# The low part of every split issued before the functions that hang on a step's end

## The chip, the cores and the metric

The kernel runs on one core of one Trainium2 chip. The metric is the time of one execution on the device in microseconds, as the median of several runs. A profiled execution of the same program gives the trace that all rows here are read from.

## What is computed

The reference is a decoder trunk of two layers over 256 tokens of width 2048, in float32. The first layer mixes with a gated recurrence (RG-LRU) and causal pooling, the second with sparse attention in three branches; both then have a squared-ReLU MLP of width 8192 and a gated addition of a per-layer embedding, and a norm closes the whole. Cut to what the change touches:

```python
hn = rmsnorm(h, ln_mlp_g[i])
h = h + jnp.square(jax.nn.relu(hn @ mlp_w_up[i])) @ mlp_w_down[i]
gate = jax.nn.sigmoid(rmsnorm(h, ln_ple_g[i]) @ ple_w_gate[i])
h = h + gate * (p[i] @ ple_w_proj[i])
...
return rmsnorm(h, ln_final_g)      # after both layers
```

The mixers are `ab_mixer` (projection, causal convolution of four taps, two gates per head, a scan over time, pooling, projection) and `nsa_mixer` (projection, compression of keys and values, softmax over the compressed, selected and windowed keys, projection).

## The kernel before

Every matmul multiplies float32 numbers as two parts of a rounded type: a **high part**, which ScalarE makes by copying 128 x 1024 raw weights into the rounded type (`emit_hi`, L204), and a **low part**, which VectorE makes by subtracting the high part from the raw weights (`emit_lo`, L211). TensorE then runs three products for each pair of tiles: high x high and high x low of the activations, and low x high (L704, L705, L706 in the large sets; L294, L298, L299 in the others). The weights, 1 MB a load, come in by SyncE's queue.

The program is a list of **steps**. A step takes half a load (two tiles of 128 rows), and `run()` (from L249) writes the code for one step after the other. The order of the code is the order on each engine: nothing is rescheduled. For step s it issues, before the change, in this order: sums of weights for step s+4 where a set needs them (`emit_sum`), the high part for step s+2, the low part of step s if it isn't there yet, the step's matmuls (`fn`), then the functions that were put down for the end of this step, and last the low part for step s+2.

`after(n, fn)` puts a function down for the end of the n-th step from now; everything that turns a finished set of matmuls into the next input goes that way: the additions, relus and squares of the MLP, the transposes, the scans, the softmax, the Tanhs. A step of twelve matmuls is TensorE's unit of time, and a function put down for the next step comes one step later on every engine.

The large sets (`mm_set`) do a matrix of 128 x 8 by 512 in a Strassen-like scheme: products p over sums of blocks, with results kept in 8 PSUM banks, and some products moved out to SBUF tiles (`u` and `big`, L760 to L770) in the course of the set. `column()` gives the last product of a set; its `by_n` tells that one of the two column blocks n is complete. At the end of an **up set** of the MLP (`up_out`, from L925; 16 of them, two layers of four quarters of two halves) there are two column blocks of 512, n = 0 and 1. For each: `adds` (L932, VectorE, two operations, from PSUM into `u` and `big`), `relu` (L936 and L938 on ScalarE, two relus and two squares), and then `back`, the transposes on TensorE (L807) that read the squares, `u` and `big` by turns, followed by copies and subtractions that split them.

The **gate sets** of the second layer (`gate`, from L1006) end in `last`: two Tanhs on ScalarE (L1023), on VectorE an addition with product and an addition to the stream `h` for each token tile t (L1027, L1028), a square with a running sum on ScalarE (L1067), and products by the gain of the final norm (L1031). The very last call of it is followed by `finish`, which takes the root of the mean square (L1072) and writes the output. Ahead of the last squares an activation of one column, `warm` (L1025), makes the table of the root load early.

## Time and profile before

| what | value |
|---|---|
| median of 3 runs | 2303.78 us (2302.41 to 2306.06) |
| the profiled execution | 2306.73 us |
| its span in the trace | 2304.7 us |
| mean granted clock of TensorE | 0.996 of full speed |
| TensorE (PE) busy | 2277.0 us, 99%, 11510 matmuls |
| weight loads (PEld) busy | 1933.8 us, 84% |
| VectorE (DVE) busy | 1734.8 us, 75% |
| ScalarE (ACT) busy | 1315.6 us, 57% |
| chain that ended last | TensorE 97%, VectorE 1%, ScalarE 1% |

Read it from the top: TensorE is the engine that sets the time, and the chain of work that ended last runs on it almost all through. The other two are busy for much of the time beside it, VectorE most of all with low parts (L211, 817 + 128 of them, 1098 us), but their busy time is not on the path. Each engine runs its own list in order and halts at an instruction whose input isn't there; what stands behind it halts too.

### The profile page before, as it was taken

To read this page: it belongs to the slowest core of one execution; us is meant where nothing else is said; L and a number is where in the kernel's file an instruction comes from. 1 tells how busy PE (TensorE), PEld (TensorE's weight loads), DVE (VectorE), ACT (ScalarE), POOL (GpSimd) and SP (SyncE) were. 2 spreads that over 40 slices of the span, in tenths; PEclk is the share of its full clock that TensorE was granted. 3 is DMA by queue.
4 is the path that set the end of the run, shared out by engine and by line. 5 is a ranking of instruction groups with operands and counts; after the bars stand their busy time and mean duration, and the time that the engine had idled before them with its cause. 6 is when DMAs were issued, how large, how long until landed. Compare 5 with 4: busy or idle time off the path is not lost.

```text
span 2304.7 us, 30201 instructions
## 1 busy us (share of the span) xinstructions
PE 2277.0 (99%) x11510; PEld 1933.8 (84%) x11510; DVE 1734.8 (75%) x2365; ACT 1315.6 (57%) x1903; POOL 14.5 (1%) x42
## 2 busy tenths in 40 slices
PE   8999999999999999999999999999999999999997
PEld 8998888888888888889889988888888888888875
DVE  6786688788788787756775675687877877877864
ACT  6665465565565565665564554566456556556563
POOL 2000000000000000000000000000000000000000
PEclk9999999999999999999999999999999999999998
DMA  7545556556555555555775224555555555555553
GB/s 258 212 157 184 197 182 213 189 182 212 190 183 209 193 181 201 199 175 201 268 263 178 83 85 162 187 187 197 201 187 197 200 186 198 201 185 198 207 175 111
DMA packets 69537, 436.56 MB, mean 189 GB/s; under 512 B 9872, under 2 KB 14352, under 8 KB 18448
## 3 DMA queue, kind: packets, MB, share of 16 engines
q1 hardware_dynamic: 64832, 427.90, 53.3%
q10 hardware_dynamic: 4560, 6.74, 0.9%
q8 instruction: 90, 1.47, 0.3%
q14 instruction: 55, 0.45, 0.1%
HBM read 432.51 MB, written 2.10 MB: 189 GB/s over the span
## 4 chain that ended last, share of the span: by engine, by line
PE 97%; DVE 1%; ACT 1%; DMA 0%; issue 0%; SPq 0%; DVEq 0%; ACTq 0%
PE ps L706 25%; PE ps L704 25%; PE ps L705 25%; PE ps L294 11%; PE ps L298 3%; PE ps L807 2%; PE ps L299 1%; PE ps L1378 1%; PE ps L1168 1%; DVE lo L211 0%; DMA raw<-in_ab_w_in 0%; PE ps L1320 0%; PE ps L1318 0%; PE ps L960 0%; PE ps L587 0%; PE ps L1321 0%
## 5 line engine op out<-in xcount | busy, mean ns | idle before, releaser
L204 ACT ACTIVATE hi<-raw 128x1024 fp32r<-128x1024 f32 (+1 forms) x817 | 819.0, 1015 | 475.5 <-PE ps L705 390.0
L211 DVE TENSOR_TENSOR lo<-raw,hi 128x1024 fp32r<-128x1024 f32 (+1 forms) x817 | 941.2, 1165 | 193.9 <-ACT hi L204 193.4
L704 PE MATMUL ps<-hi,big 128*128 128x512 f32 x2496 | 978.3, 392 | 0.0
L706 PE MATMUL ps<-lo,big 128*128 128x512 f32 x2496 | 973.2, 390 | 4.8 <-DVE lo L211 4.8
L705 PE MATMUL ps<-hi,big 128*128 128x512 f32 x2496 | 973.0, 390 | 0.0
L706 PEld LDWEIGHTS ps<-lo,big 128*128 128x128 f32 x2496 | 469.4, 188 | 103.9 <-DVE lo L211 6.1
L705 PEld LDWEIGHTS ps<-hi,big 128*128 128x128 f32 x2496 | 469.5, 188 | 95.6
L704 PEld LDWEIGHTS ps<-hi,big 128*128 128x128 f32 x2496 | 469.3, 188 | 95.3
L294 PE MATMUL ps<-big,hi 128*128 128x256 f32 x1408 | 265.8, 290 | 6.7 <-ACT hi L204 6.4
L204 ACT ACTIVATE hi<-big 128x1024 fp32r<-128x1024 f32 x128 | 135.8, 1061 | 212.2 <-PE ps L705 198.6
L211 DVE TENSOR_TENSOR lo<-big,hi 128x1024 fp32r<-128x1024 f32 x128 | 156.5, 1223 | 120.2 <-ACT hi L204 120.2
L294 PEld LDWEIGHTS ps<-big,hi 128*128 128x128 f32 x1408 | 223.9, 194 | 9.1 <-ACT hi L204 6.4
L294 PE MATMUL ps<-big,lo 128*128 128x256 f32 x704 | 201.0, 286 | 1.2 <-DVE lo L211 1.2
L294 PEld LDWEIGHTS ps<-big,lo 128*128 128x128 f32 x704 | 136.3, 194 | 1.8 <-DVE lo L211 1.8
L298 PE MATMUL ps<-big,hi 128*128 128x512 f32 x320 | 113.7, 398 | 0.0
L299 PE MATMUL ps<-big,lo 128*128 128x256 f32 x320 | 89.7, 280 | 0.6 <-DVE lo L211 0.5
L735 DVE TENSOR_TENSOR big<-raw 128x1024 f32<-128x1024 f32 x64 | 77.9, 1218 | 0.0
L298 PEld LDWEIGHTS ps<-big,hi 128*128 128x128 f32 x320 | 60.1, 188 | 14.2
L950 DVE TENSOR_TENSOR big<-ps,big 128x512 fp32r<-128x512 f32 x64 | 41.1, 684 | 36.6 <-ACT big L946 36.6
L299 PEld LDWEIGHTS ps<-big,lo 128*128 128x128 f32 x320 | 60.4, 189 | 2.0 <-DVE lo L211 1.5
L410 ACT ACTIVATE big<-ps,gains 128x256 fp32r<-128x256 f32 x80 | 31.2, 471 | 42.6 <-PE ps L807 42.6
L866 DVE SCALAR_TENSOR_TENSOR big<-ps,gains,big 128x256 fp32r<-128x256 f32 x80 | 33.2, 476 | 25.1 <-ACT big L410 20.4
(249 smaller groups left out, 1514.5 us busy)
## 6 DMA issues: line engine op xcount, KB each, us to landing
raw<-in_mlp_w_up SPq DMA_DIRECT2D x128, 1024.0 KB, 4.9
raw<-in_mlp_w_down SPq DMA_DIRECT2D x128, 1024.0 KB, 4.9
raw<-in_c_w_in SPq DMA_DIRECT2D x36, 1024.0 KB, 4.9
raw<-in_ple_w_gate SPq DMA_DIRECT2D x32, 1024.0 KB, 4.9
raw<-in_ab_w_in SPq DMA_DIRECT2D x20, 1024.0 KB, 4.9
raw<-in_ab_w_out SPq DMA_DIRECT2D x16, 1024.0 KB, 4.9
raw<-in_c_w_out SPq DMA_DIRECT2D x16, 1024.0 KB, 4.9
raw<-in_c_cmp_w_k SPq DMA_DIRECT2D x8, 1024.0 KB, 5.0
```

Source lines behind the costliest of these rows:

```text
L204: act.activation(halves[s]["hi"][:, k, :w], halves[s]["src"][:, k, :], AF.Copy)
L211: dve.tensor_tensor(lo[:, k, :w], src[:, k, :], halves[s]["hi"][:, k, :w].bitcast(F32), op=OP.subtract)
L294: pe.matmul(b, lhsT=wt[:, kk, cols], rhs=x[:, x0:x0 + T], start=first and n == 0 and j % 2 == 0, stop=last and n == 2, skip_group_check=True)
L298: pe.matmul(b, lhsT=hi[:, kk, cols], rhs=x, start=first, stop=False, skip_group_check=True)
L299: pe.matmul(b[:, T:], lhsT=lo[:, kk, cols], rhs=x[:, :T], start=False, stop=last, skip_group_check=True)
L704: pe.matmul(b, lhsT=x_hi, rhs=hi[:, n, :], start=r not in begun, stop=False, skip_group_check=True)
L705: pe.matmul(b, lhsT=x_lo, rhs=hi[:, n, :], start=False, stop=False, skip_group_check=True)
L706: pe.matmul(b, lhsT=x_hi, rhs=lo[:, n, :], start=False, stop=end, skip_group_check=True)
L735: dve.tensor_tensor(t, raw[:, 0::3, :], raw[:, 1:2, :].to_broadcast([P, 2, 512]), op=OP.add)
L807: pe.transpose(b[:, j, t * P:(t + 1) * P], of(t, i // 2, (2 * i + j) % 4), ident)
L866: dve.scalar_tensor_tensor(X(k)[:, T:], scratch(banks, i)[:, j], gain(k), X(k)[:, :T].bitcast(F32), op0=OP.mult, op1=OP.subtract)
L950: dve.tensor_tensor(Hs[n2][:, k:k + 2, T:], scratch(banks, i), Hs[n2][:, k:k + 2, :T].bitcast(F32), op=OP.subtract)
```

## The change

Three things change. In `run()` the low part for step s+2 is issued right behind the matmuls of step s, ahead of the functions put down for the step's end; these are then called until none is left for this step, so that one of them can put down another for the same step. In `column()` the call of `by_n` becomes such a function. And in the gate sets of the second layer the work of `last` is dealt out: the second column block comes two steps behind the first instead of one, the additions of token tile 1 come one step behind those of tile 0, and the products by the gain later or with them; the early load of the root's table is taken out.

```diff
--- before.py
+++ after.py
@@ -255,10 +255,11 @@
             splits("hi", ahead)
             splits("lo", s)
             fn(halves[s]["hi"], halves[s]["lo"])
+            splits("lo", ahead)
             now = state["step"]
-            for f in later.pop(now, []):
-                f()
-            splits("lo", ahead)
+            while now in later:
+                for f in later.pop(now):
+                    f()
             state["step"] += 1
             halves[s].clear()
         while later:
@@ -776,7 +777,7 @@
                     for t in range(2):
                         product(PLAIN[t][n], A(p, k, t), hi, lo, k, k == 1 and p == order[-1])
                 if p == order[-1]:
-                    by_n(n, [acc_of(PLAIN[t][n]) for t in range(2)])
+                    after(0, lambda: by_n(n, [acc_of(PLAIN[t][n]) for t in range(2)]))
             return fn
 
         for i, p in enumerate(order):
@@ -1021,21 +1022,30 @@
                 end = n2 == 1 and n == 1
                 for t in range(2):
                     act.activation(W[t][:, n], banks[t], AF.Tanh, scale=HALF[:, t:t + 1])
-                if end:
-                    act.activation(warm, epsb, AF.Sqrt)
-                for t in range(2):
+
+                def add(t):
                     dve.scalar_tensor_tensor(W[t][:, n], W[t][:, n], 1.0, eb(t, n), op0=OP.add, op1=OP.mult)
                     dve.tensor_tensor(hb(t, n), hb(t, n), W[t][:, n], op=OP.add)
                     last_square(t, n2, n)
-                for t in range(0 if end else 2):
+
+                def times_gain(t):
                     dve.tensor_tensor(hg(t, n), hb(t, n), gb(n), op=OP.mult)
                 if end:
+                    add(0)
+                    add(1)
                     finish()
+                    return
+                for t in range(2):
+                    after(t, lambda t=t: add(t))
+                    if n2 == 0:
+                        after(4 + 2 * n + t, lambda t=t: times_gain(t))
+                    else:
+                        after(t, lambda t=t: times_gain(t))
 
             def post(w, banks):
                 if l == 1:
                     for n in range(2):
-                        after(n, lambda n=n: last(n, [banks[t][n] for t in range(2)]))
+                        after(2 * n, lambda n=n: last(n, [banks[t][n] for t in range(2)]))
                     return
                 W = wtiles()
 
```

VectorE at the end of an up set, before; `lo` is a low part, named by its tile's number, with the raw weights and the high part that it reads, and L932 are the additions of block 0 and then of block 1:

```order
L761 TENSOR_TENSOR u_3250<-ps_1968,u_3250 128x512
L211 TENSOR_TENSOR lo_3255<-raw_3154,hi_3242 128x1024
L765 SCALAR_TENSOR_TENSOR big_2268<-big_2268,u_3250 128x512
L766 TENSOR_TENSOR u_3250<-u_3250,big_2268 128x512
L211 TENSOR_TENSOR lo_3275<-raw_3177,hi_3259 128x1024
L770 SCALAR_TENSOR_TENSOR big_2268<-big_2268 128x512
L932 TENSOR_TENSOR u_3250<-ps_2277,u_3250 128x512
L932 TENSOR_TENSOR big_2268<-ps_2282,big_2268 128x512
L211 TENSOR_TENSOR lo_3298<-raw_3177,hi_3277 128x1024
L932 TENSOR_TENSOR u_3250<-ps_2281,u_3250 128x512
L932 TENSOR_TENSOR big_2268<-ps_2289,big_2268 128x512
L211 TENSOR_TENSOR lo_3330<-raw_3230,hi_3302 128x1024
```

VectorE at the same place, with the change (the additions are L933 there):

```order
L211 TENSOR_TENSOR lo_3250<-raw_3154,hi_3242 128x1024
L762 TENSOR_TENSOR u_3252<-ps_1968,u_3252 128x512
L211 TENSOR_TENSOR lo_3273<-raw_3177,hi_3259 128x1024
L766 SCALAR_TENSOR_TENSOR big_2268<-big_2268,u_3252 128x512
L767 TENSOR_TENSOR u_3252<-u_3252,big_2268 128x512
L211 TENSOR_TENSOR lo_3291<-raw_3177,hi_3277 128x1024
L771 SCALAR_TENSOR_TENSOR big_2268<-big_2268 128x512
L933 TENSOR_TENSOR u_3252<-ps_2277,u_3252 128x512
L933 TENSOR_TENSOR big_2268<-ps_2282,big_2268 128x512
L211 TENSOR_TENSOR lo_3316<-raw_3230,hi_3302 128x1024
L933 TENSOR_TENSOR u_3252<-ps_2281,u_3252 128x512
L933 TENSOR_TENSOR big_2268<-ps_2289,big_2268 128x512
```

Each low part has moved up by one group of functions, so that one now stands between the two pairs of additions, and it reads `hi_3302`. On ScalarE, where that high part is made, the order is that of before; with the change, from the relus of block 0 to the squares of block 1:

```order
L937 ACTIVATE u_3252<-u_3252 128x512
L937 ACTIVATE big_2268<-big_2268 128x512
L939 ACTIVATE u_3252<-u_3252 128x512
L939 ACTIVATE big_2268<-big_2268 128x512
L204 ACTIVATE hi_3302<-raw_3230 128x1024
L937 ACTIVATE u_3252<-u_3252 128x512
L937 ACTIVATE big_2268<-big_2268 128x512
L939 ACTIVATE u_3252<-u_3252 128x512
L939 ACTIVATE big_2268<-big_2268 128x512
```

Nothing moved here: `hi_3302` stands behind the relus and squares of block 0, and ahead of those of block 1.

VectorE at the end of the second layer's first gate set (`h_79` is the stream, L1027 and L1028 the additions), before:

```order
L1027 SCALAR_TENSOR_TENSOR u_18224<-u_18224,big_17865 128x512
L1028 TENSOR_TENSOR h_79<-h_79,u_18224 128x512
L1027 SCALAR_TENSOR_TENSOR big_12316<-big_12316,big_17865 128x512
L1028 TENSOR_TENSOR h_79<-h_79,big_12316 128x512
L1031 TENSOR_TENSOR big_17867<-h_79,big_17866 128x512 x2
L211 TENSOR_TENSOR lo_18235<-raw_18124,hi_18210 128x1024
L1027 SCALAR_TENSOR_TENSOR u_18224<-u_18224,big_17865 128x512
L1028 TENSOR_TENSOR h_79<-h_79,u_18224 128x512
L1027 SCALAR_TENSOR_TENSOR big_12316<-big_12316,big_17865 128x512
L1028 TENSOR_TENSOR h_79<-h_79,big_12316 128x512
L1031 TENSOR_TENSOR big_17867<-h_79,big_17866 128x512 x2
L211 TENSOR_TENSOR lo_18263<-raw_18158,hi_18239 128x1024
```

and with the change:

```order
L211 TENSOR_TENSOR lo_18208<-raw_18124,hi_18194 128x1024
L211 TENSOR_TENSOR lo_18224<-raw_18124,hi_18210 128x1024
L1027 SCALAR_TENSOR_TENSOR u_18226<-u_18226,big_17865 128x512
L1028 TENSOR_TENSOR h_79<-h_79,u_18226 128x512
L211 TENSOR_TENSOR lo_18248<-raw_18158,hi_18234 128x1024
L1027 SCALAR_TENSOR_TENSOR big_12316<-big_12316,big_17865 128x512
L1028 TENSOR_TENSOR h_79<-h_79,big_12316 128x512
L211 TENSOR_TENSOR lo_18267<-raw_18158,hi_18253 128x1024
L1027 SCALAR_TENSOR_TENSOR u_18226<-u_18226,big_17865 128x512
L1028 TENSOR_TENSOR h_79<-h_79,u_18226 128x512
L211 TENSOR_TENSOR lo_18290<-raw_18192,hi_18276 128x1024
L1027 SCALAR_TENSOR_TENSOR big_12316<-big_12316,big_17865 128x512
```

The first low part stands ahead of the additions, a low part follows each further pair, and the products L1031 (L1032 with the change) stand further back.

ScalarE at the program's end, before:

```order
L1023 ACTIVATE u_18517<-ps_12325,rs_81 128x512
L1023 ACTIVATE big_12316<-ps_12330,rs_81 128x512
L1067 ACTIVATE jk_82,ssq_80<-h_79 128x512 x2
L1023 ACTIVATE u_18517<-ps_12329,rs_81 128x512
L1023 ACTIVATE big_12316<-ps_12337,rs_81 128x512
L1025 ACT_TABLE_LOAD
L1025 ACTIVATE warm_92<-epsb_88 128x1
L1067 ACTIVATE jk_82,ssq_80<-h_79 128x512 x2
L1072 ACTIVATE rs_81<-rs_81,epsb_88 128x2
L1080 ACTIVATE big_17867<-big_17867,rs_81 128x768 x2
```

and with the change:

```order
L1024 ACTIVATE u_18519<-ps_12325,rs_81 128x512
L1024 ACTIVATE big_12316<-ps_12330,rs_81 128x512
L1077 ACTIVATE jk_82,ssq_80<-h_79 128x512 x2
L1024 ACTIVATE u_18519<-ps_12329,rs_81 128x512
L1024 ACTIVATE big_12316<-ps_12337,rs_81 128x512
L1077 ACTIVATE jk_82,ssq_80<-h_79 128x512 x2
L1082 ACT_TABLE_LOAD
L1082 ACTIVATE rs_81<-rs_81,epsb_88 128x2
L1090 ACTIVATE big_17867<-big_17867,rs_81 128x768 x2
```

The load of the table has moved from behind the last Tanhs to behind the last squares, right ahead of the root.

## Rows read from the trace of the kernel before

**Rows 1.** The page's first part: TensorE's busy time and share of the span.

```profile
PE 2277.0 (99%) x11510; PEld 1933.8 (84%) x11510; DVE 1734.8 (75%) x2365; ACT 1315.6 (57%) x1903; POOL 14.5 (1%) x42
```

**Rows 2.** TensorE's waits: who waited for whom, us in total, times, longest.

```profile
PE ps L706 <- DVE lo L211: 4.8, 3, 2.1
PE ps L294 <- DVE lo L211: 1.2, 1, 1.2
PE ps L1356 <- DVE big L1352: 0.5, 1, 0.5
PE ps L299 <- DVE lo L211: 0.5, 1, 0.5
```

**Rows 3.** Timeline of TensorE at an up set's end: start, us, engine, line, operation.

```profile
345.42 0.27 PE L807 MATMUL ps<-ident,big 128*128 128x128 f32 x1
...
349.03 0.27 PE L807 MATMUL ps<-ident,big 128*128 128x128 f32 x1
```

**Rows 4.** Timeline of VectorE at the same end; in brackets, idle before and releaser.

```profile
336.73 0.69 DVE L761 TENSOR_TENSOR u<-ps,u 128x512 f32<-128x512 f32 x1 [0.88 <-PE ps L706]
337.34 1.22 DVE L211 TENSOR_TENSOR lo<-raw,hi 128x1024 fp32r<-128x1024 f32 x1
338.47 0.69 DVE L765 SCALAR_TENSOR_TENSOR big<-big,u 128x512 f32<-128x512 f32 x1
...
341.61 0.69 DVE L932 TENSOR_TENSOR u<-ps,u 128x512 f32<-128x512 f32 x1
```

**Rows 5.** Timeline of ScalarE at the same end.

```profile
336.95 2.01 ACT L204 ACTIVATE hi<-raw 128x1024 fp32r<-128x1024 f32 x2
...
343.98 0.62 ACT L938 ACTIVATE big<-big 128x512 f32<-128x512 f32 x1
344.50 1.04 ACT L204 ACTIVATE hi<-raw 128x1024 fp32r<-128x1024 f32 x1
...
347.01 0.62 ACT L938 ACTIVATE big<-big 128x512 f32<-128x512 f32 x1
```

**Rows 6.** Timeline of TensorE at the second layer's first gate set's end.

```profile
2233.00 0.39 PE L704 MATMUL ps<-hi,big 128*128 128x512 f32 x1
...
2235.72 0.39 PE L704 MATMUL ps<-hi,big 128*128 128x512 f32 x1
...
2242.15 0.50 PE L706 MATMUL ps<-lo,big 128*128 128x512 f32 x1 [2.07 <-DVE lo L211]
...
2246.82 0.39 PE L704 MATMUL ps<-hi,big 128*128 128x512 f32 x1
```

**Rows 7.** Stretches: us, TensorE busy (count), granted clock, DMA share, GB/s.

```profile
18.20:19.00 0.80, 0.80 (x6) 0.50 1.01 394
...
2244.00:2244.80 0.80, 0.80 (x3) 0.50 0.71 113
```

**Rows 8.** Timelines of VectorE and ScalarE in the recurrence.

```profile
94.58 0.43 DVE L543 TENSOR_TENSOR big<-big 128x256 f32<-128x256 f32 x1 [0.95 <-ACT big L540]
...
94.45 2.00 ACT L204 ACTIVATE hi<-raw 128x1024 fp32r<-128x1024 f32 x2
```

**Rows 9.** Timelines of VectorE and ScalarE at the last attention heads.

```profile
1383.71 1.28 DVE L1352 TENSOR_SCALAR big<-big,mz 128x128 f32<-128x128 f32 x6
...
1383.15 1.99 ACT L204 ACTIVATE hi<-raw 128x1024 fp32r<-128x1024 f32 x2
```

**Rows 10.** Timelines of TensorE and ScalarE at the end of the program.

```profile
2284.61 0.39 PE L705 MATMUL ps<-hi,big 128*128 128x512 f32 x1
...
2290.68 0.52 PE L706 MATMUL ps<-lo,big 128*128 128x512 f32 x1
...
2291.23 0.69 ACT L1023 ACTIVATE big<-ps,rs 128x512 f32<-128x512 f32 x1 [0.48 <-PE ps L706]
2291.94 1.28 ACT L1025 ACT_TABLE_LOAD   x1
...
2295.03 0.30 ACT L1072 ACTIVATE rs<-rs,epsb 128x2 f32<-128x2 f32 x1 [0.23 <-DVE rs L376]
```

## The prediction

> **What bounds the kernel now.** I read the busy shares first, then the list of waits, then the timelines of the places where the order of work changes. TensorE is busy 2277.0 us of the 2304.7 us span [rows 1], so an edit can gain little except where TensorE stands. Outside the ramp at the start and the tail its list of waits is short [rows 2]: three waits for a low part at L706 (4.8 us together), one at L294 (1.2), one for the scaled probabilities at L1356 (0.5), one at L299 (0.5). So nearly every result that VectorE and ScalarE make comes in time, and what the reader must ask of each move is not how long VectorE works but how near to its deadline the work was that now stands behind a low part.
>
> The pace: twelve matmuls, one plain step, go from 2233.00 to 2235.72, 2.72 us, 0.2268 each [rows 6]. A low part holds VectorE for 1.13 us, from its start at 337.34 to that of the next operation at 338.47 [rows 4]; a high part takes ScalarE 1.04 [rows 5].
>
> The profiled execution took 2306.73 us, the span and 2.03 around it; the median of the timed runs, 2303.78, is 2.95 below it. My sum is of differences, so I read it from the trace and put it on the median. A difference under 0.2%, 4.6 us, can't be told from none.
>
> **The change part by part.** No instruction is added but one load of a table that trades its place; TensorE's order stays. What moves is VectorE's: each low part goes ahead of the functions that hang on its step's end.
>
> *The end of an up set, 16 times (two layers, four quarters, two halves).* The code's order for VectorE becomes: additions for column block 0, low part, additions for block 1. The low part needs its high part, and that one stands on ScalarE behind the two relus and two squares of block 0, which need the additions of block 0. So block 1, which waited for none of this, now waits for all of it. By times: in the trace VectorE idles 0.88 us ahead of L761 at 336.73 [rows 4], so the first low part that is moved fits there for nothing. The next can't start at 337.34 as a low part did there: its high part is the first of the pair that begins at 336.95 on ScalarE and takes until 338.0 [rows 5], so it starts at about 338.03, 0.69 later, and everything up to the additions of block 0 moves from 341.61 to 342.30. The squares of block 0 end 2.99 us after the additions' start (341.61 to 344.60, the second square beginning at 343.98 and lasting 0.62), so now at 345.29; the transposes that need the last of them stood at 345.42 [rows 3]: just in time. The high part then ends 0.94 later, at 346.23; the low part runs 346.27 to 347.40; only there do the additions of block 1 start, and 2.99 later, at 350.39, their last square is done. The second transpose of that block, the first to read it, stood at 349.03 [rows 3]. It starts at 350.42: 1.39 us lost on TensorE, whose queue is in order. I find no cover: the other 15 sets have the same three orders, and the matmuls behind the transposes are TensorE's own. In the first set of each layer two more small operations stand in the chain, 1.86 there. Sum: 14 x 1.39 + 2 x 1.86 = **+23.2**. Bounds: 10 (if the high part gets to ScalarE some 0.8 earlier than I think) to 30 (if the transposes of block 0 come late too).
>
> *The recurrence, near 95 us.* The scans' products start at 94.58, right behind the square root on ScalarE; the high parts come behind that root, from 94.45 as a pair [rows 8]. The low part that now stands ahead ends near 96.6, so scans and all behind them come 2.1 later, and VectorE doesn't rest before the convolution that TensorE then takes up. Estimate from these: **+1.6**, between 0 and 2.1.
>
> *The attention's heads.* TensorE already waits for the scaling at L1356 [rows 2]. At the last pair the scaling begins at 1383.71 [rows 9]; a low part is put ahead of it whose high part begins at 1383.15, behind the exponentials, and so ends near 1384.2. Low part to 1385.4, the scaling's two small operations again, scaling at 1385.8: +2.1, all of it on TensorE, since the wait had no slack. The other heads have some slack; I put 1.2 on them. **+3.3**, between 1.5 and 6.
>
> *Start and 1115 us.* Here TensorE waits for the low part itself, 1.2 and 0.5 [rows 2]; it now stands ahead of two conversions of x or of a few additions. **-0.7** and **-0.5**, bounded by nothing and the whole wait.
>
> *The second layer's gate set, 2236 to 2247.* From 2235.72 to 2246.82 stand 27 matmul intervals, 11.10 us where 27 x 0.2268 = 6.12 would do: 4.98 lost, of which 2.07 is the one wait before 2242.15 [rows 6] and a good third the half-speed stretch that follows it, in which the granted clock is 0.50, the 1.2 GHz level [rows 7]. In the changed order the low parts of both waits stand ahead of the additions, so these waits go. But the dealt-out additions now take turns with low parts as in the up set: high part 1.04, low part 1.13, two additions 1.3, square 0.7 make 4.2 us a turn, where TensorE's step takes 2.72. Three turns are covered by the lead that the first low part gains; at the fourth and fifth TensorE waits 0.5 and 1.55. So 2.05 stay lost: **-2.9**, between 0 and -4.9.
>
> *The end.* Ten intervals from 2284.61 to 2290.68, 6.07 instead of 2.27 [rows 10], for the same reason; with the low part early the last matmul starts at 2286.88, and the last Tanh, at 2291.23 before, at 2287.30. VectorE's four operations behind the Tanhs, about 0.69 each [rows 4], end at 2290.09, the last square at 2290.85. Now the load of the root's table, 1.28, begun at 2291.94 before while VectorE worked [rows 10], stands bare ahead of the root: 2292.15 against 2295.03. **-2.9**; the lost cover costs 0.5 of it net, since in the old place the load held up a square. Bounds -1.5 and -4.2. The Trainium skill ("ScalarE: Activation LUTs", What ACT_TABLE_LOAD costs) has 1.28 us for the load, which this trace's 1.28 confirms, and adds a drain of about 1.38, which no row here shows; by it the tail would gain 1.5 and not 2.9, and the forecast would be 1.4 higher.
>
> Sum: 23.2 + 1.6 + 3.3 - 0.7 - 0.5 - 2.9 - 2.9 = **+21.1**; 2303.8 + 21.1 = **2324.9 us**.
>
> **The rivals.** *Only the gains come.* If ScalarE's order didn't bind, because the high part were ready before the additions of block 0 end, a low part ahead of block 1 would cost its 1.13, and block 1 has 1.4 to spare (its last square, from 347.01 on and as long as that at 343.98, ends at 347.63; its transpose stands at 349.03 [rows 3, 5]). Then the 16 sets cost nothing, the recurrence and the heads likewise, and the four gains stay: -7.0, **2296.8**. It decides from the point at which the high part stands no more than 0.3 us behind its place before. Against it: ScalarE shows the high part at 344.50, directly behind the square of block 0 at 343.98 and 1.04 long [rows 5], and the change leaves ScalarE's order there as it is. The Trainium skill ("Perfetto Trace Analysis", Optimization Strategy) says to find the gaps on the engine that limits and to make what blocks them start sooner; the change does that for the gaps at L706, and by that rule alone this case would be the result.
>
> *The clock falls at each new gap.* The 2.07 us wait was followed by a stretch at 0.50 [rows 6, 7], which cost some 1.7, the good third of the 4.98; the waits of 0.5 at L1356 were not. A gap of 1.4 lies between. If each of the 16 were followed so, 16 x 1.7 = +27.2: **2352.1**. For it: the gap of 1.2 at the start [rows 2] was followed by such a stretch too [rows 7]. Against: each of these new gaps has full matmul work on both sides, where the start is a ramp.
>
> *Half the price.* If in some sets the chain starts earlier, as the additions of block 0 find their banks done before VectorE gets there, the sets cost 0 to 12 together: 2302 to 2314, about **2308**.
>
> **How the numbers follow.** Forecast (own range 2314 to 2334): 64%, since the chain closes over two engines whose orders are both fixed. Only the gains: 17%. Half the price: 12%. Clock at most gaps: 7%. Slower by over 0.2%: 64 + 7 + half of the 12 = 0.77; within: the other half, 0.06; faster: 0.17. The range takes in the first three cases in the main: 2295 to 2335 and leaves out the clock's.
>
> **What would show it.** Right: TensorE's list of waits has a new line at L807, from the squares at the up set's end, 16 or 32 times, some 22 to 25 us together; the last square of block 1 begins 7.5 us after the additions of block 0 instead of 5.4; VectorE's low part between the pairs of additions waits about 2.7 us for its high part; the waits at L706 fall from 4.8 below 3; the root's table load stands bare in the chain at the end. Wrong: no such line at L807, with the low part between the additions starting at once (only the gains); gaps there of 1.4 followed by matmuls 0.43 apart (the clock); gaps of 0.5 or less (half the price).

## The result, and the profile after

The changed kernel takes 2336.23 us in the median of 4 runs (2335.48 to 2337.29), against 2303.78 before: 32.45 us more, a ratio of 1.014 with a 95% interval of 1.0128 to 1.0152. The forecast was slower, by 21.1 us, with a range that ended at 2335.0. The sign and the main mechanism were right; the size was short by a third, and the time lies 1.2 us above the range.

TensorE is busy for 98% of a span of 2333.7 us, and its list of waits has changed. The list for the kernel after, to be held against [rows 2] (TensorE's line numbers are higher: L294 is now L295, L706 is L707, L807 is L808, L1356 is L1366); the columns are us in total, times, longest:

```profile
PE ps L808 <- ACT u L939: 12.9, 16, 0.8
PE ps L295 <- ACT hi L204: 7.5, 1, 7.5
PE ps L808 <- ACT big L939: 3.4, 18, 0.2
PE ps L1366 <- DVE big L1362: 2.6, 1, 2.6
PE ps L519 <- DVE big L514: 1.6, 1, 1.6
PE ps L1216 <- issue: 1.4, 1, 1.4
PE ps L300 <- DVE lo L211: 1.3, 2, 0.8
PE ps L1178 <- DVE lo L211: 1.1, 1, 1.1
PE ps L707 <- DVE lo L211: 1.0, 2, 0.5
```

The new first line is the one that was foretold: 16 waits at the transposes for a square on ScalarE. The waits at L707 fell from 4.8 to 1.0. The head's wait grew from 0.5 to 2.6. In the compression of the second layer's keys and values stand two lines that the forecast doesn't have, L1178 and L1216, and one that it expected to shrink: L300, which is L299 in [rows 2], grew from 0.5 to 1.3.

This is the same up set's end as in [rows 3 to 5]. VectorE (timeline: start, duration, engine, line, operation, in brackets idle time before and releaser):

```profile
338.98 0.68 DVE L762 TENSOR_TENSOR u<-ps,u 128x512 f32<-128x512 f32 x1
340.12 1.23 DVE L211 TENSOR_TENSOR lo<-raw,hi 128x1024 fp32r<-128x1024 f32 x1 [0.45 <-ACT hi L204]
...
344.32 0.68 DVE L933 TENSOR_TENSOR u<-ps,u 128x512 f32<-128x512 f32 x1
344.93 0.68 DVE L933 TENSOR_TENSOR big<-ps,big 128x512 f32<-128x512 f32 x1
348.29 1.23 DVE L211 TENSOR_TENSOR lo<-raw,hi 128x1024 fp32r<-128x1024 f32 x1 [2.69 <-ACT hi L204]
349.43 0.68 DVE L933 TENSOR_TENSOR u<-ps,u 128x512 f32<-128x512 f32 x1
```

ScalarE at the same place:

```profile
345.04 0.64 ACT L937 ACTIVATE u<-u 128x512 f32<-128x512 f32 x1 [4.01 <-DVE u L933]
...
346.69 0.62 ACT L939 ACTIVATE big<-big 128x512 f32<-128x512 f32 x1
347.22 1.04 ACT L204 ACTIVATE hi<-raw 128x1024 fp32r<-128x1024 f32 x1
350.15 0.63 ACT L937 ACTIVATE u<-u 128x512 f32<-128x512 f32 x1 [1.89 <-DVE u L933]
```

TensorE's transposes of block 1:

```profile
351.95 0.33 PE L808 MATMUL ps<-ident,u 128*128 128x128 f32 x1 [0.81 <-ACT u L939]
352.47 0.33 PE L808 MATMUL ps<-ident,big 128*128 128x128 f32 x1 [0.19 <-ACT big L939]
```

Read it as a ring. VectorE's low part at 348.29 waited 2.69 us for the high part; ScalarE's high part at 347.22 stood behind the squares; the squares had waited for VectorE's additions at 344.32. So the additions of block 1 start 5.1 us after those of block 0 where 2.3 would do, and TensorE, which has no other work, waits. The gap is in two pieces, 0.81 and 0.19, because the first transpose reads `u` and the second `big`. The lag of 1.43 us that the set leaves is more than this 1.00: these transposes follow each other 0.11 us apart in the trace of before, each while the last one still runs, and one that follows a gap has none to overlap (here the second starts 0.52 behind the first).

A low part stood between the two pairs before the change as well. In the trace of before:

```profile
342.81 1.22 DVE L211 TENSOR_TENSOR lo<-raw,hi 128x1024 fp32r<-128x1024 f32 x1
343.94 0.69 DVE L932 TENSOR_TENSOR u<-ps,u 128x512 f32<-128x512 f32 x1
```

The first pair began at 341.61 [rows 4], so the second came 2.33 us later with a low part in between, one whose high part was the second of the pair that began at 336.95 [rows 5]. The change adds no work there. It puts another low part into the place, the next one, whose high part is made behind block 0's squares.

Over the whole program VectorE's waits of this kind went up from 313.6 us in 242 waits to:

```profile
DVE lo L211 <- ACT hi L204: 535.4, 349, 7.1
```

### The profile page after: what moved, and what is told of

Read it like the earlier page. It is cut to its first block, busy times and chain, and to the rows that moved or that the text cites. A ratio compares the mean times of both kernels' runs of the same rounds, so it can differ in the third digit from the quotient of the medians.

```text
span 2333.7 us, 30191 instructions
## 1 busy us (share of the span) xinstructions
PE 2282.9 (98%) x11510; PEld 1929.5 (83%) x11510; DVE 1730.8 (74%) x2365; ACT 1316.6 (56%) x1902; POOL 14.8 (1%) x42
## 4 chain that ended last, share of the span: by engine, by line
PE 88%; ACT 5%; DVE 5%; issue 1%; DMA 1%; SPq 0%; ACTq 0%; DVEq 0%
PE ps L705 22%; PE ps L706 22%; PE ps L707 22%; PE ps L295 10%; PE ps L299 3%; DVE lo L211 3%; PE ps L300 2%; PE ps L1388 1%; ACT hi L204 1%; PE ps L808 1%; PE ps L1178 1%; ACT u L937 1%; DVE u L933 1%; ACT big L937 1%; ACT big L939 1%
## 5 line engine op out<-in xcount | busy, mean ns | idle before, releaser
L707 PE MATMUL ps<-lo,big 128*128 128x512 f32 x2496 | 972.2, 389 | 1.1 <-DVE lo L211 1.0
L706 PE MATMUL ps<-hi,big 128*128 128x512 f32 x2496 | 971.6, 389 | 0.0
L707 PEld LDWEIGHTS ps<-lo,big 128*128 128x128 f32 x2496 | 468.6, 188 | 100.5 <-DVE lo L211 2.9
L706 PEld LDWEIGHTS ps<-hi,big 128*128 128x128 f32 x2496 | 468.9, 188 | 95.4
L295 PE MATMUL ps<-big,hi 128*128 128x256 f32 x1408 | 263.7, 289 | 8.0 <-ACT hi L204 7.5
L295 PEld LDWEIGHTS ps<-big,hi 128*128 128x128 f32 x1408 | 222.3, 193 | 10.2 <-ACT hi L204 7.5
L295 PE MATMUL ps<-big,lo 128*128 128x256 f32 x704 | 199.8, 284 | 0.0
L295 PEld LDWEIGHTS ps<-big,lo 128*128 128x128 f32 x704 | 135.4, 192 | 0.2 <-DVE lo L211 0.2
L299 PE MATMUL ps<-big,hi 128*128 128x512 f32 x320 | 114.0, 399 | 0.7 <-ACT hi L204 0.7
L300 PE MATMUL ps<-big,lo 128*128 128x256 f32 x320 | 89.7, 280 | 1.3 <-DVE lo L211 1.3
L937 ACT ACTIVATE u<-u 128x512 f32<-128x512 f32 x32 | 20.3, 633 | 95.3 <-DVE u L933 95.3
L299 PEld LDWEIGHTS ps<-big,hi 128*128 128x128 f32 x320 | 60.1, 188 | 15.4 <-ACT hi L204 1.1
L300 PEld LDWEIGHTS ps<-big,lo 128*128 128x128 f32 x320 | 60.3, 189 | 2.5 <-DVE lo L211 2.0
L742 DVE TENSOR_TENSOR big<-big,raw 128x512 f32<-128x512 f32 x64 | 44.3, 692 | 2.2
```

Of the source, the lines that this page charges most:

```text
L295: pe.matmul(b, lhsT=wt[:, kk, cols], rhs=x[:, x0:x0 + T], start=first and n == 0 and j % 2 == 0, stop=last and n == 2, skip_group_check=True)
L299: pe.matmul(b, lhsT=hi[:, kk, cols], rhs=x, start=first, stop=False, skip_group_check=True)
L300: pe.matmul(b[:, T:], lhsT=lo[:, kk, cols], rhs=x[:, :T], start=False, stop=last, skip_group_check=True)
L706: pe.matmul(b, lhsT=x_lo, rhs=hi[:, n, :], start=False, stop=False, skip_group_check=True)
L707: pe.matmul(b, lhsT=x_hi, rhs=lo[:, n, :], start=False, stop=end, skip_group_check=True)
L742: dve.tensor_tensor(t[:, 1], t[:, 0], raw[:, 2], op=OP.add)
```

## Where the time went, place by place

TensorE runs the same 11510 matmuls in the same order in both kernels, so the n-th of one trace can be held against the n-th of the other, and the lag between them grows only where one of them loses time. From the profiled execution of before (2306.73 us) to that of after (2335.48 us) it grows by 28.8 us:

| place (us in the trace of before) | forecast | measured |
|---|---|---|
| start, to 22 | -0.7 | -2.5 |
| recurrence near 50 | 0 | +0.9 |
| recurrence near 103 | +1.6 | +1.8 |
| 16 up sets | +23.2 | +23.7 |
| two places in the MLPs, 930 and 2162 | 0 | +0.7 |
| compression, 1113 to 1194 | -0.5 | +5.2 |
| attention heads, 1373 to 1389 | +3.3 | +4.3 |
| gate set, 2235 to 2252 | -2.9 | -2.5 |
| the end | -2.9 | -2.8 |
| sum | 21.1 | 28.8 |

Each of 14 up sets lost 1.41 to 1.44 us, and the first of each layer 1.86. The 28.8 of the two traces stand against 32.45 of the medians, because the trace of before lies 2.95 above its median and that of after 0.75 below. Where the 2.95 come from is told below, under "From the trace to the median".

## The experiments

**The up sets undone.** In the two steps at the end of each up set the functions come first again, and the low part last:

```diff
+    late = set()
...
-            splits("lo", ahead)
             now = state["step"]
+            if now not in late:
+                splits("lo", ahead)
             while now in later:
                 for f in later.pop(now):
                     f()
+            splits("lo", ahead)
...
             def post(w, banks):
                 W = w or wtiles()
+                late.update((state["step"], state["step"] + 1))
```

> The changed kernel, but in the two steps at the end of each of the 16 up sets the low part stands behind the functions of the step's end again, as before the change. Theory (at these places VectorE's additions of block 1 wait for a low part, whose high part waits on ScalarE for the squares of block 0): the 16 waits of TensorE at the second block's transposes go, 14 x 1.43 + 2 x 1.86 = 23.7 us, so 2312.5, and the list of waits has no line at L808 over 1 us. Rival (VectorE is delayed by low parts standing early everywhere, wherever in the program): less than half of it comes back, over 2324.

Measured: 2313.38 us (2313.04 to 2313.59), 1.0042 of before, interval 1.0027 to 1.0057. Of 2336.2, 22.9 us are gone, the wait at the transposes is off the list, and no up set's matmuls lag any longer; every other place of the table keeps its loss (the compression has 1.5 more here, for a stretch at half clock that the trace of the changed kernel doesn't have, see below). The theory holds for the place and the price, not yet for the cause.

**High parts ahead too.** The one line that breaks the ring: in each step the next high part is issued behind the low part, ahead of the functions.

```diff
             splits("lo", ahead)
+            splits("hi", ahead + 1)
             now = state["step"]
```

> The changed kernel, and in every step the high part of the step after the next-but-one is issued right behind that low part, so ahead of the relus and squares that hang on the step's end. The low part that stands between the two pairs of additions then finds its high part done. Theory (the price is the wait for the high part, not VectorE's 1.13 us of low part): the 23.7 us of the up sets go, with 0 to 8 more from the other places where VectorE waited for a high part: 2304 to 2312. Rival (the low part ahead of the additions costs by its own time): 2330 or more.

Measured: 2305.30 us (2303.59 to 2307.03), 1.0007 of before (0.9997 to 1.0016). 31 us go although VectorE's order is still that of the changed kernel. The up sets cost nothing but 0.35 and 0.70 in the first of each layer. But the kernel is no faster than before. Against the trace of before it gets 8.8 at the gate set and the end (-5.0 and -3.8) and gives back 5.8 elsewhere, 2.1 of it in the compression and 1.2 in the heads, and 1.0 at the bare load of the table. A high part now stands ahead of an exponential or a root there; that this is what costs was not tried by itself.

**High parts ahead in the up sets alone.** The same line, in the two steps at each up set's end and nowhere else:

```diff
+            now = state["step"]
             splits("lo", ahead)
-            now = state["step"]
+            if now in late:
+                splits("hi", ahead + 1)
             while now in later:
```

> The changed kernel, but in the two steps at each up set's end alone the next high part is issued ahead of the relus and squares; the low part stays between the pairs of additions. Theory (it is the wait for the high part that costs): 22 to 24 us of 2336.2 go, 2312 to 2314.5, with no row at the set's transposes over 1 us but the first set of each layer. Rival (what brought the time down with high parts ahead everywhere was some other place): less than 12 us go, over 2324.

Measured: 2312.81 us (2311.70 to 2315.63), 1.0039 of before (1.0026 to 1.0053): 23.4 us go, as with the order undone. VectorE at the same up set's end (L937 are the additions here, L212 the low part, L205 the high part):

```profile
343.00 0.68 DVE L937 TENSOR_TENSOR u<-ps,u 128x512 f32<-128x512 f32 x1
343.60 0.68 DVE L937 TENSOR_TENSOR big<-ps,big 128x512 f32<-128x512 f32 x1
344.20 1.22 DVE L212 TENSOR_TENSOR lo<-raw,hi 128x1024 fp32r<-128x1024 f32 x1
345.33 0.69 DVE L937 TENSOR_TENSOR u<-ps,u 128x512 f32<-128x512 f32 x1
```

and ScalarE:

```profile
340.58 1.06 ACT L205 ACTIVATE hi<-raw 128x1024 fp32r<-128x1024 f32 x1 [0.88 <-PE ps L709]
343.72 0.63 ACT L941 ACTIVATE u<-u 128x512 f32<-128x512 f32 x1 [2.08 <-DVE u L937]
```

The low part still stands between the pairs of additions, and now starts at once, since its high part was made at 340.58 in time in which ScalarE waited anyway. From pair to pair it is 2.33 us again, as in the trace of before. So it is the wait that costs: this is what the first rival needed to be true, and in the changed kernel it wasn't.

**The gate edits alone.** The low parts stay behind the functions in every step; the rest of the change is kept.

```diff
-            splits("lo", ahead)
             now = state["step"]
             while now in later:
                 for f in later.pop(now):
                     f()
+            splits("lo", ahead)
```

> The kernel before with the gate edits alone: the second layer's additions dealt out, the last column's function put at the step's end, the table's load at the root; every low part stands behind the functions of its step as before. Theory (the low parts at the two gate ends were late because all four operations and the products by the gain stood ahead of them; dealt out, only two stand ahead): most of the gain of the gate set and the end comes without moving a low part, 4 to 6 us, so 2298 to 2300. Rival (that gain hangs on the low part being ahead): within 1.5 us of 2303.8, or slower.

Measured: 2298.26 us (2297.64 to 2299.15), 0.9976 of before (0.9966 to 0.9985): faster than both kernels. Against the trace of before the gate set gets 4.9 us back, all that it lost, and the end's matmuls 3.3; about 1.5 of each is the half-speed stretch that followed the wait in that trace. The medians show 5.6 and not the 7 that these make less the bare load; why is told below, under "From the trace to the median". The part of the change that was to bring the low parts forward isn't needed even for the waits at L706. VectorE at the gate set's end in this kernel:

```profile
2231.15 0.69 DVE L1027 SCALAR_TENSOR_TENSOR u<-u,big 128x512 f32<-128x512 f32 x1 [4.75 <-ACT u L1024]
2231.88 0.69 DVE L1028 TENSOR_TENSOR h<-h,u 128x512 f32<-128x512 f32 x1
2232.49 1.22 DVE L211 TENSOR_TENSOR lo<-raw,hi 128x1024 fp32r<-128x1024 f32 x1
2233.62 0.68 DVE L1027 SCALAR_TENSOR_TENSOR big<-big 128x512 f32<-128x512 f32 x1
```

and the same operations in the changed kernel, with low parts ahead:

```profile
2266.66 0.69 DVE L1027 SCALAR_TENSOR_TENSOR u<-u,big 128x512 f32<-128x512 f32 x1 [2.03 <-ACT u L1024]
2267.38 0.69 DVE L1028 TENSOR_TENSOR h<-h,u 128x512 f32<-128x512 f32 x1
2269.81 1.22 DVE L211 TENSOR_TENSOR lo<-raw,hi 128x1024 fp32r<-128x1024 f32 x1 [1.74 <-ACT hi L204]
2270.96 0.68 DVE L1027 SCALAR_TENSOR_TENSOR big<-big 128x512 f32<-128x512 f32 x1
```

Dealt out, a low part behind two additions is early enough and finds its high part done; a turn takes 2.47 us, less than TensorE's 2.72 [rows 6]. With the low part ahead each turn takes 4.30, and the ring is there again.

**The moved low part alone.** The other half of the change, on the kernel before:

```diff
+            splits("lo", ahead)
             now = state["step"]
             for f in later.pop(now, []):
                 f()
-            splits("lo", ahead)
```

> The kernel before with the low part moved ahead in every step and nothing else. Theory: it pays the up sets (23.7), the compression near 1113 to 1194 (5), the heads (4), the recurrence (2.7), and gets the waits at L706 back at the two gate ends, about what the whole change gets: 2334 to 2339. Rival (the dealt-out additions of the gate are what costs or gains): outside of that by 3 us or more.

Measured: 2339.04 us (2337.59 to 2340.63), 1.0153 of before (1.0138 to 1.0168), at the top of what was expected and 0.04 past it. All losses of the table are there. The gate set gets 3.0 back, more than the 2.5 of the whole change. At the end its matmuls get 1.4 back where the whole change gets 3.8, and not by a shorter wait: TensorE stands 2.04 us there, as it stood 2.05 before. The trace of before has a stretch at half clock behind that wait and this one has none; this is the 1.4. So at the end the low part alone gains nothing.

**The kernel before, a second look.**

> The kernel before, unchanged, for a second profile of its start. In the first profile TensorE waited 1.2 us near 16 for a low part whose weights landed late, and a stretch at half clock followed; the changed kernel and the gate edits alone show neither. Theory (that was the landing of the first loads in that execution, not the order): this profile shows the start without it or with another size, and TensorE's matmuls from 25 us on stand 0.5 to 3 us earlier than in the first. Rival (the order makes the wait): again about 1.2 us near 16 and the same time after it.

Measured: 2305.35 us. TensorE's wait for a low part is there again, 0.8 us, later, and with no half-speed stretch behind it. From 22 us to the end no place differs by 0.3 us from the first trace, but the matmuls stand 1.4 us earlier. The fourth high part on ScalarE (the second of full size), in the first trace of before, in this one, and in the changed kernel, each in a fence of its own:

```profile
13.43 1.06 ACT L204 ACTIVATE hi<-raw 128x1024 fp32r<-128x1024 f32 x1 [2.88 <-DMA raw<-in_ab_w_in]
```

```profile
12.44 1.06 ACT L204 ACTIVATE hi<-raw 128x1024 fp32r<-128x1024 f32 x1 [1.60 <-DMA raw<-in_ab_w_in]
```

```profile
11.92 1.06 ACT L204 ACTIVATE hi<-raw 128x1024 fp32r<-128x1024 f32 x1 [1.18 <-DMA raw<-in_ab_w_in]
```

It waits for the landing of a load, and that differs by 1.0 us between these two executions of one program. The changed kernel's landing came 1.5 earlier than the first trace's, and this is most of the -2.5 that it seems to gain at the start. The first trace's poor start explains 1.4 of the 2.95 by which it lies above its median.

The order has a part in it, too, and the rival is half right. The five traces in which the low part stands behind the functions all have TensorE wait for a low part before 22 us, 0.8 to 2.0 us together (1.8 for the gate edits alone, of which the expectation said that they show none); the six with the low part ahead and the high part left in its place have no such wait. From that fourth high part to the matmul that stands at 22.05 in the first trace it is 8.6 us there, 8.25 to 8.27 in the other four of the five, and 7.6 in the changed kernel (7.6 to 8.25 in the six). So the changed kernel gains about 0.7 at the start by its order.

**The second layer's mixer undone as well.** On top of the up sets undone:

```diff
-            if now not in late:
+            if now not in late and not late_all:
...
     add_hook(open1)
+    add_hook(lambda: late_all.append(1))
...
+    add_hook(late_all.clear)
     X5 = new_x()
```

> As the run with the up sets undone (2313.4), and all through the second layer's mixer, too, the low part stands behind the functions of its step. Theory (the low part ahead costs 5 to 7 us in the compression near 1113 to 1194 and 4 in the heads, each by a function of VectorE waiting for the next high part): 11 us go, 2302 to 2303.5, and the waits at the heads' transposes are those of before (0.5 and 0.3). Rival (these waits only follow from the up sets' delays or from loads): over 2308.

Measured: 2302.44 us (2301.73 to 2302.96), 0.9991 of before (0.9982 to 1.0000): 10.9 us go, where the table has 9.5 for compression and heads together. The waits at the heads' transposes are those of before, 0.5 and 0.3. The 1.4 above the table are the stretch at half clock near 1178 that the trace with the up sets undone has and the table's trace hasn't. So the compression's loss is the low part's, too. VectorE in the changed kernel there, where the Gelu's steps alternate with low parts:

```profile
1180.26 0.42 DVE L1197 TENSOR_TENSOR t<-ps,t 128x256 f32<-128x256 f32 x1
1182.17 1.22 DVE L211 TENSOR_TENSOR lo<-raw,hi 128x1024 fp32r<-128x1024 f32 x1 [1.49 <-ACT hi L204]
...
1184.18 0.42 DVE L618 SCALAR_TENSOR_TENSOR t<-t 128x256 f32<-128x256 f32 x1
1186.03 1.23 DVE L211 TENSOR_TENSOR lo<-raw,hi 128x1024 fp32r<-128x1024 f32 x1 [1.43 <-ACT hi L204]
1187.17 0.41 DVE L1205 SCALAR_TENSOR_TENSOR t<-t 128x256 f32<-128x256 f32 x1
```

Each low part waits about 1.45 us for a high part that ScalarE makes behind the activation (L614, L1202) that VectorE's step before has fed: the ring of the up sets, with smaller operations. It stands where 3.2 of the 5.2 us are lost. At 1113 and 1193, 1.0 each, the traces show no ring: a low part ahead of VectorE's work waits there for its high part (1.50 us at 1112.71, 1.61 at 1207.61 in the changed kernel), and what follows goes on without a rest, but late.

**Two blocks one step apart.** The gate edits alone, with `after(n, ...)` in place of `after(2 * n, ...)`:

```diff
-                        after(2 * n, lambda n=n: last(n, [banks[t][n] for t in range(2)]))
+                        after(n, lambda n=n: last(n, [banks[t][n] for t in range(2)]))
```

> The gate edits alone, but the second column block again one step behind the first instead of two. Theory (what helped at 2236 to 2247 is that the additions are dealt out by token tiles, so that a low part follows each pair; two blocks one step apart put the second block's pair back on the same step): half or more of the 4.9 us of that place is lost again, 2300 to 2303. Rival (dealing out alone does it): within 1 us of 2298.3.

Measured: 2298.19 us (2297.86 to 2298.91), 0.9973 of before (0.9962 to 0.9984), the same as with two steps, and the gate set gets the same 4.9 us back. The theory fell: the spacing of the blocks does nothing. What helps is that two operations in place of four, and no products by the gain, stand ahead of a low part. How much of it is the dealing out of the additions and how much the later products was not tried apart.

**The table early again.** The gate edits alone, and `warm` back behind the last Tanh:

```diff
                 if end:
+                    act.activation(warm, epsb, AF.Sqrt)
                     add(0)
```

> The gate edits alone (2298.3 in its run), and the load of the root's table again right behind the last Tanh, ahead of the last two squares. Theory (in that kernel 1.28 us of load stands bare between the last square and the root, and behind the Tanh it has VectorE's additions beside it): the root comes 0.6 to 1.3 us earlier, so 2297.0 to 2297.7. Rival (the load holds up the squares by as much as it saves): within 0.3 us of the gate edits alone.

Measured: 2296.86 us (2296.25 to 2297.31), 0.9966 of before (0.9953 to 0.9978). From the last matmul's start to the root the trace has 4.32 us, where the gate edits alone have 5.40. ScalarE at the end of the changed kernel, where the load stands bare:

```profile
2322.97 0.19 ACT L1077 ACTIVATION_READ_ACCUMULATOR jk<-h 128x1 f32 x1
2323.18 1.28 ACT L1082 ACT_TABLE_LOAD   x1
2324.47 0.30 ACT L1082 ACTIVATE rs<-rs,epsb 128x2 f32<-128x2 f32 x1
```

and with the table early:

```profile
2281.96 1.28 ACT L1034 ACT_TABLE_LOAD   x1
2283.26 0.20 ACT L1034 ACTIVATE warm<-epsb 128x1 f32<-128x1 f32 x1
2283.37 0.61 ACT L1078 ACTIVATE jk<-h 128x512 f32<-128x512 f32 x1
...
2285.15 0.30 ACT L1083 ACTIVATE rs<-rs,epsb 128x2 f32<-128x2 f32 x1 [0.23 <-DVE rs L377]
```

**The start too.** The same, with low parts ahead in the first six steps alone:

```diff
             now = state["step"]
+            if now < 6:
+                splits("lo", ahead)
             while now in later:
```

> The gate edits with the table's load early (2296.9 in its run), and in the first six steps the low part ahead. Theory (at the start, where TensorE does wait for a low part, being ahead helps by what two conversions of x take, 0.9, unless the weights land late): 0 to 0.9 faster, 2296.0 to 2296.9, at the edge of what can be told. Rival (the start is set by the landing of the loads): the same as without, within 0.3.

Measured: 2295.60 us (2295.43 to 2296.20), 0.9964 of before (0.9950 to 0.9977), the best of all here. It is 1.26 us below the run without this line, but the two were not run together and their intervals against before overlap nearly wholly. Of the 1.0 us that the trace shows for the start, half is the landing of the load (the fourth high part at 11.75 instead of 12.27) and half stands behind it, with no wait for a low part where the other trace has 1.1. That the start gains about half a microsecond by it is likely, and the times alone don't prove it.

## Why the prediction was right and where it failed

*The up sets: right, and by the stated mechanism.* 23.2 was forecast, 23.7 measured. The chain was read from durations of before and the new order alone. The forecast had VectorE's wait for the high part at about 2.7 (2.69 in the trace), and the loss at 1.39 and 1.86 a set (1.43 and 1.86). The list of waits has 16.3 us for it and not the 22 to 25 that were to show it, since it counts idle time alone. The experiments with the high part ahead show the cause: same order on VectorE, no loss.

*The clock: right for the up sets, wrong at the heads.* The stretch around a gap of an up set in the changed kernel, and the one behind it (us, TensorE busy, granted clock, DMA share, GB/s):

```profile
350.00:353.40 3.40, 2.40 (x15) 1.00 0.00 0
353.40:357.00 3.60, 3.60 (x18) 1.00 0.40 96
```

TensorE stood for 1.00 of 3.40 us and the granted clock stayed at 1.00, the 2.4 GHz level; 16 gaps of this size didn't bring one stretch at half clock. But in the same trace the wait at the heads did:

```profile
1405.22 0.30 PE L1366 MATMUL ps<-ident,big 128*128 128x128 f32 x1 [2.60 <-DVE big L1362]
```

```profile
1407.00:1410.40 3.40, 3.40 (x11) 0.50 0.38 159
```

The forecast's 2.1 for the last pair of heads is what the wait cost, 2.07; another 1.6 us went in the stretch at 0.50, the 1.2 GHz level, behind it. The rival let the clock fall at the new gaps of the sets; the prediction never asked it of the wait at the heads, which it had itself made 2.6 long. The other heads took 0.7 and not 1.2. So the heads measure +4.3, 1.0 over the forecast, by the clock.

In the traces of this case such a stretch came behind eight of the nine waits of 2.04 to 2.60 us, and not behind every shorter one: the wait of 1.4 at L1216 was followed by one in three traces and not in the changed kernel's.

*The compression: the step that failed.* The term "start and 1115 us" took for granted that where TensorE waits for a low part, issuing it earlier makes it come earlier, and put -0.5 there; nothing was put on the rest of the compression. It measures +5.2. The question that the same text asks of the up sets, what the high part of the moved low part stands behind, wasn't asked there: at 1182 and 1186 VectorE waits about 1.45 us for a high part that stands behind an activation. The wait at 1115, which was to shrink, is still 0.5, with a new one of 1.1 ahead of it. Of the 11.3 us between forecast and medians, 5.7 are this term.

*Terms that stood in no sum, or were a little off.* The recurrence has a second convolution, near 50, with +0.9, and the MLPs two places of +0.35; neither was in the sum. With +0.2 near 103 this makes 1.8. The gate set gained 2.5 and not 2.9: the turns take 4.30 to 4.35 us, where 4.2 were reckoned. With the sets and the end this is another 1.0.

*The start: right in size.* Of the -2.5 that the traces show, the order makes about 0.7, which is what was forecast. The other 1.8 are the first trace's late landing (1.5) and what else its start lost. They made the traces come out nearer to the forecast than the change deserves.

*From the trace to the median: a step of the prediction that failed, too.* The sum was read from one trace and put on the median. In that trace TensorE has a stretch at 0.50 at three places, behind the waits at 17.0, at 2242.15 and at 2287.05, and the -2.9 for the gate set and the -2.9 for the end each include about 1.5 us for getting one back (at the end the same wait costs 3.8 with the stretch behind it and 2.4 without). Most runs of before seem to have fewer. Its 45 later runs group by their mean granted clock: seven at 0.998 took 2301.8 to 2303.5 us, twenty at 0.997 2302.9 to 2304.5, seventeen at 0.996 2304.3 to 2305.6, and one at 0.995 2306.6. The profiled execution, 2306.73 at 0.996, is slower than all of these, and the median stands among the 0.997. So in a median run there was less to get back, and the medians lie 3.7 further apart than the traces. Which run had which stretch isn't on record, so this much is argued. The traces account for the other 7.7 of the 11.3: 5.7 + 1.0 + 1.8 + 1.0, less the 1.8 of the start.

*The end: right against the trace.* The matmuls got back the 3.8 that were foretold, and the bare table load took 1.0 of it: -2.8 against -2.9. (The prediction's text has the lost cover at 0.5; its own sum, 3.8 less 2.9, at 0.9.) The Trainium skill ("ScalarE: Activation LUTs", What ACT_TABLE_LOAD costs) has a drain of about 1.38 us with each load, besides the 1.28. In the trace after, the root starts at 2324.47, 1.29 after its load at 2323.18, and the load starts 0.02 behind the end of the operation ahead of it, so no such drain stands there; and putting the load early gained 1.08 in the trace, less than the load alone. The sum without the drain was the right one.

*The rivals.* "Only the gains" was wrong for this change, but its mechanism, with the high part done in time, is what the two kernels with high parts ahead do. It gave the low part between the pairs a price of 1.13 out of 1.4 us to spare; one stood there before the change as well, so there was no such price. The Trainium skill ("Perfetto Trace Analysis", Optimization Strategy) says to make what blocks the limiting engine start sooner, or complete faster. The waits at L706 did shrink from 4.8 to 1.0 in the whole change. But the moved low part alone leaves 2.6 of them, and took the low parts ahead of work that TensorE needed more; with the gate edits alone the same waits shrink to 0.2. In its range the prediction gave the side of higher cost too little room: places that weren't read had no bounds in it.

## What to carry to other kernels

Before an operation is moved ahead on an engine that runs in order, ask what its input stands behind on the engine that makes it: if that depends on the work it is moved past, the two engines take turns, and each move costs a full round trip and not the operation's own time. Shortening what stands ahead of a late operation, here by dealing four additions out over two steps and the products behind them later, gets the gain without the ring. The durations of one trace with the new order were enough to price a turn of such a ring to within 0.2 us at the places that were read; the places that weren't read are where the forecast failed most. And one trace has the waits and the clock of one execution: before a gain read from it is put on a median, see whether other runs have the same mean granted clock.

## What the runs showed of the hardware that was not expected

The landing of the first loads differs between executions of one program by 1.0 us (a high part at 13.43 and at 12.44 in two traces of before), and a span taken from one profile carries that. A gap of 1.0 us in a stretch of full matmul work, 16 times, left the granted clock at 1.00. The same wait can have a stretch at 0.50 behind it in one execution and not in another: 2.05 us at the end of the program had one in both traces of before, and 2.04 at the same place had none with the low part alone, which made 1.4 us. The times of the kernel before go with the mean granted clock of each run, from 0.998 (2301.8 to 2303.5 us) to 0.995 (2306.6).
